# A hybrid decoder step on one core: the kept rows of the cache copied in eight DMAs behind heads 4 to 11, instead of one behind head 7

## The chip, the cores and the metric

The kernel runs on one core of one Trainium2 chip. The time is the device time of that core in microseconds (us), the median of several runs. Engines are named as the profile names them: PE (TensorE), PEld (its weight loads), DVE (VectorE), ACT (ScalarE), POOL (GpSimd), SP (SyncE, which here only issues DMAs). Heads are counted as in the code, from 0, so the twelfth head is head 11.

## The reference, cut to what matters

One step of a decoder of two layers over 512 prompt tokens and 8 x 8 sample tokens. The first layer is a gated linear recurrence with 16 heads, the second a sliding-window attention over one shared K/V. The part that the change is about is the last output: the K/V cache of the eight sample sequences (8 x 128 rows of 512 numbers), shifted by the eight new rows.

```python
def reference(...):
    hp, sp = hgrn2_layer(hp, s_zero, ...)          # layer 0, prompt: 16 heads, 128 x 128 states
    hs, ss = hgrn2_layer(hs, state_hgrn[0], ...)   # layer 0, sample
    kv_p = shared_kv(hp, norm_kv, w_kv)
    kv_s = shared_kv(hs, norm_kv, w_kv)
    ...                                            # layer 1: attention over kv_p, kv_s and the cache
    kv_window_sample = jnp.concatenate([cache_kv_window, kv_s], axis=1)[:, -128:]
```

Of each sequence 120 rows (240 KB) of `cache_kv_window` stay, 8 rows up in the output; they are copied from DRAM to DRAM and nothing in the kernel reads the copy.

## The kernel before, in words

**Stages.** The first layer works head by head. `head_main(h)` multiplies the normed tokens by four 1024 x 128 blocks of `w_in_a` (products `pf`, `pq`, `pi`, `pg`, each of 48 matmuls 128 x 288 on PE, line 233) and ends with the transposes `pvt` and `pvs` (lines 649 and 655). `head_rec(h)` does the recurrence of head h: small matmuls `pa` and `smg`, transposes `pkt` and `pks`, state products `pu`, the chain of states `S` (ACT, then three times DVE, line 856), outputs `poT` and `psO`, sample states `pus`. `woven` writes `head_rec(h)` between the products of `head_main(h + 1)`. Where h is 4, 8 or 12, eight output products `po` of the four heads before (`out_product`, four weight blocks, 24 x 2 matmuls for each product) stand ahead of them.

**Weights.** Every block goes through `split_weights`: one DMA of 512 KB into one of three buffers `raw` (line 198), a cast to `whi` on ACT (line 205), the difference `wlo` on DVE (line 209), then the matmuls. A `raw` buffer is free again when its `wlo` is made.

**What sets the order.** The code gives dependences and priorities. A planner of the framework fixes each engine's instruction order when the kernel is built, with its own estimate of how long every instruction and every DMA takes. On the chip each engine then works through that order and waits where an operand is late. All DMAs of the first layer are issued by SP in one queue, in order; their ends are told by eight semaphores in turn, so an issue can carry a wait for an older DMA that used the same semaphore.

**The copy.** In `head_rec`, after the store of the head's prompt state (`kept`, line 860), head 7 (`CACHE`) issues one DMA (line 864) for the kept rows of all eight sequences, `co[:, : P - DL, :]` from `ci[:, DL:, :]`. `tc.issue_after(kept.ins)` places it right behind the store on SP. After it stand the loads of the next sample states `S0` (line 868, three half tiles of 256 KB) and the stores of the finished ones (line 924).

Of the kernel before, what the change touches and what calls it, by code (L numbers as in the profile page):

```python
# [19 lines left out]
P = 128  # L20
# [3 lines left out]
DB = 8  # L24
DL = 8
# [28 lines left out]
EXTRA = 4  # L54
LAG = 2
SGP = True
CACHE = 7
W = 192
SILU_POOL = True
SCALE = "vpvp"  # L60
# [23 lines left out]
def yoco_kernel(  # L84
# [26 lines left out]
    act, dve, pool, pe, sp = nc.scalar, nc.vector, nc.gpsimd, nc.tensor, nc.sync  # L111
# [416 lines left out]
    ci = cache_kv_window.rearrange("b s k g d -> b s (k g d)")  # L528
    co = kvw_sample.rearrange("b s k g d -> b s (k g d)")

    with ExitStack() as actx:
# [153 lines left out]
        def head_rec(h, st, outs):  # L685
# [172 lines left out]
                        )  # L858
                    Ss.append(S)
            kept = sp.dma_start(st_prompt[0, 0, h], Ss[-1])  # L860
            if h == CACHE:

                with tc.issue_after(kept.ins):
                    sp.dma_start(co[:, : P - DL, :], ci[:, DL:, :])
            S0 = []
            for half in range(2):
                t = wk.tile([P, 4, P], F32, tag="S0", name=f"S0{half}_{h}", bufs=3)
# [94 lines left out]
        for h in range(NH):  # L962
            nxt, chunks, n = {}, [], 0
            if h % 4 == 0 and h:
                chunks.append(out_product(w_out_a, h - 4, outs))
                outs = []
                n += 8
            if h + 1 < NH:
                chunks.append(head_main(h + 1, nxt))
                n += 12  # L970
            else:
                chunks.append(out_product(w_out_a, NH - 4, outs[:FILL]))
                n += 8
            woven(head_rec(h, st, outs), itertools.chain(*chunks), n)
            for make in {5: (prompt_mask,), 6: (sample_mask,), 7: (sink_rows,)}.get(h, ()):
                make()
            st = nxt
# [600 lines left out]
```

## Time and profile before

| what | value |
|---|---|
| time, median of 3 runs | 1152.77 us (1152.27 to 1153.73) |
| time of the profiled execution | 1152.44 us |
| its span, first to last instruction | 1150.6 us |
| mean granted TensorE clock | 0.987 |
| PE busy | 1105.9 us (96%) |
| DVE busy | 857.6 us (75%) |
| ACT busy | 749.4 us (65%) |
| DMA traffic | 123.19 MB, mean 107 GB/s |

The span is the profiled execution from its first to its last instruction; its time is 1.8 us longer. The start of `pvt` (line 649) closes one head's `head_main` on PE, so the time from one `pvt` to the next is a period of the first layer, and two periods that do the same work can be held against each other. A granted clock of 1.00 is 2.4 GHz, and the lower of the two levels is 1.2 GHz.

### The profile page before, as it was taken

To read this page: it belongs to the slowest core of one execution; us is meant where nothing else is said; L and a number is where in the kernel's file an instruction comes from. 1 tells how busy PE (TensorE), PEld (TensorE's weight loads), DVE (VectorE), ACT (ScalarE), POOL (GpSimd) and SP (SyncE) were. 2 spreads that over 40 slices of the span, in tenths; PEclk is the share of its full clock that TensorE was granted. 3 is DMA by queue.
4 is the path that set the end of the run, shared out by engine and by line. 5 is a ranking of instruction groups with operands and counts; after the bars stand their busy time and mean duration, and the time that the engine had idled before them with its cause. 6 is when DMAs were issued, how large, how long until landed. Compare 5 with 4: busy or idle time off the path is not lost.

```text
span 1150.6 us, 27472 instructions
## 1 busy us (share of the span) xinstructions
PE 1105.9 (96%) x10937; PEld 1072.6 (93%) x10937; DVE 857.6 (75%) x2090; ACT 749.4 (65%) x1748; POOL 265.9 (23%) x311
## 2 busy tenths in 40 slices
PE   5999999999999999999999989899999999999997
PEld 4999999998999899999999979899999998999996
DVE  8897777399985498875597887666676767576676
ACT  6677765367673467773566655678866876777665
POOL 1122221021221032121122143332332242232220
PEclk7999999999999999999999999999999999999998
DMA  5332333223233433323323223655545555554552
GB/s 157 93 113 78 104 94 113 77 79 108 71 118 107 122 87 110 89 76 107 96 71 110 86 77 92 143 137 117 132 114 126 129 128 134 126 127 113 127 111 83
DMA packets 168010, 123.19 MB, mean 107 GB/s; under 512 B 4665, under 2 KB 158314, under 8 KB 167850
## 3 DMA queue, kind: packets, MB, share of 16 engines
q1 hardware_dynamic: 160970, 96.26, 28.4%
q0 software_dynamic: 6912, 25.17, 11.6%
q8 instruction: 86, 1.41, 0.5%
q14 instruction: 42, 0.34, 0.1%
HBM read 84.06 MB, written 14.16 MB: 85 GB/s over the span
## 4 chain that ended last, share of the span: by engine, by line
PE 51%; DVE 6%; ACT 3%; issue 1%; DMA 1%; POOL 0%; DVEq 0%; POOLq 0%; ACTq 0%
PE pbg L216 8%; PE pbq L216 8%; PE po L216 6%; PE po L233 4%; PE pg L233 3%; PE pf L233 3%; PE pi L233 3%; PE pq L233 2%; PE sc L1103 2%; PE pkv L216 2%; PE pav L1186 1%; PE pz L216 1%; PE pa L802 1%; PE ptr L1154 1%; DMA wlo_o<-raw_o 1%
## 5 line engine op out<-in xcount | busy, mean ns | idle before, releaser
L205 ACT CAST whi_a<-raw_a 128x1024 fp32r<-128x1024 f32 x64 | 67.1, 1049 | 66.8 <-PE po L233 32.3
L209 DVE TENSOR_TENSOR wlo_a<-raw_a,whi_a 128x1024 fp32r<-128x1024 f32 x64 | 81.8, 1284 | 24.6 <-issue 23.2
L611 POOL TENSOR_TENSOR Xl<-Xl 128x72 f32<-128x72 f32 x80 | 49.6, 649 | 207.0 <-DVE Xl L608 205.7
L643 POOL TENSOR_TENSOR sg<-sg,lg 128x576 f32<-128x576 f32 x16 | 26.2, 1638 | 279.3 <-ACT lg L576 279.3
L1132 ACT ACTIVATE P<-P,st 128x192 f32<-128x192 f32 (+2 forms) x128 | 54.1, 424 | 38.4 <-DVE st L1127 38.3
L1141 POOL TENSOR_SCALAR P<-P,st 128x192 f32<-128x192 f32 (+1 forms) x64 | 47.9, 754 | 93.6 <-DVE st L1134 76.8
L443 DVE TENSOR_TENSOR hT<-hT,po 128x576 f32<-128x576 f32 x32 | 24.1, 754 | 51.0 <-PE po L233 50.7
L233 PE MATMUL po<-oh,whi_o 128*128 128x288 f32 x256 | 42.8, 302 | 4.4 <-ACT whi_o L205 1.9
L216 PE MATMUL po<-ohb,wlo_o 128*128 128x288 f32 x224 | 41.1, 297 | 2.2 <-DMA wlo_o<-raw_o 2.1
L667 POOL TENSOR_TENSOR vb<-vst,bmask 128x512 fp32r<-128x512 f32 x32 | 36.7, 1166 | 26.7 <-DVE vst L663 13.8
L216 PE MATMUL po<-ohb,whi_o 128*128 128x288 f32 x224 | 42.0, 302 | 0.2
L216 PE MATMUL pbq<-xhi,wlo_bq 128*128 128x256 f32 (+1 forms) x256 | 39.9, 297 | 2.4 <-DMA wlo_bq<-raw_bq 2.4
L233 PEld LDWEIGHTS po<-oh,whi_o 128*128 128x128 f32 x256 | 35.9, 188 | 6.4 <-ACT whi_o L205 2.2
L216 PE MATMUL po<-olb,whi_o 128*128 128x288 f32 x224 | 41.4, 298 | 0.5 <-DVE olb L1400 0.4
L233 PE MATMUL po<-ol,whi_o 128*128 128x288 f32 x256 | 41.4, 299 | 0.0
L233 PE MATMUL po<-oh,wlo_o 128*128 128x288 f32 x256 | 41.1, 298 | 0.0
L216 PE MATMUL pbq<-xhi,whi_bq 128*128 128x256 f32 (+1 forms) x256 | 40.5, 300 | 0.0
L216 PE MATMUL pbg<-xhi,whi_bg 128*128 128x288 f32 x256 | 40.5, 300 | 0.0
L216 PE MATMUL pbq<-xlo,whi_bq 128*128 128x256 f32 (+1 forms) x256 | 39.3, 296 | 0.0
L233 PE MATMUL pf<-xhi,wlo_a 128*128 128x288 f32 x256 | 37.5, 299 | 1.8 <-DVE wlo_a L209 1.8
L216 PE MATMUL pbg<-xhi,wlo_bg 128*128 128x288 f32 x256 | 39.1, 295 | 0.0
L233 PE MATMUL pf<-xhi,whi_a 128*128 128x288 f32 x256 | 39.1, 303 | 0.0
(390 smaller groups left out, 3676.7 us busy)
## 6 DMA issues: line engine op xcount, KB each, us to landing
raw_a<-in_w_in_a_dram SPq DMA_DIRECT2D x64, 512.0 KB
S<-in_state_hgrn_dram SPq DMA_DIRECT2D x32, 256.0 KB
out_dram<-S SPq DMA_DIRECT2D x32, 256.0 KB
raw_o<-in_w_out_a_dram SPq DMA_DIRECT2D x16, 512.0 KB
raw_bq<-in_w_in_b_dram SPq DMA_DIRECT2D x16, 512.0 KB
raw_bg<-in_w_in_b_dram SPq DMA_DIRECT2D x16, 512.0 KB
wlo_bq<-raw_bq POOLq DMA_DIRECT2D x16, 512.0 KB, 4.7
wlo_bg<-raw_bg POOLq DMA_DIRECT2D x16, 512.0 KB, 4.8
```

The lines of the kernel that those rows point to most:

```text
L205: act.copy(hi[:, :n], raw[:, :n])
L209: eng.tensor_tensor(lo[:, r], raw[:, r], hi[:, r].bitcast(F32), ALU.subtract)
L216: pe.matmul(pm[:, : c1 - c0], w[:, k * width + w0 : k * width + w0 + P], x(k)[i][:, c0:c1], start=n == 0, stop=n == len(terms) - 1,)
L233: pe.matmul(pm[:, j, :HN], w[:, k * width + c0 : k * width + c0 + P], x(k, j), start=n == 0 and k == 0, stop=n == 2 and k == nk - 1,)
L443: dve.tensor_add(h2, h2, ps2(pm))
L611: pool.tensor_tensor(X8[:, :, j : j + 1], X8[:, :, j : j + 1], X8[:, :, k : k + 1], ALU.add)
L643: (pool if SGP else dve).tensor_tensor(sg, sg, l, ALU.mult)
L667: pool.tensor_tensor(t, view(vst.bitcast(F32), [[0, 4], [1, P]], off=half * P), view(bmask, [[1, 4], [0, P]]), ALU.mult,)
L802: pe.matmul(pa[32 * j : 32 * j + ns, c, t0 : t0 + nt], keys[:, c * P + s0 : c * P + s0 + ns], queries[:, c * P + t0 : c * P + t0 + nt], st ...
L1103: pe.matmul(sc[:, hf, k0[hf] :], QS[pr][:, 2 * n + hf, :], kk[:, g, ks], start=q == 0, stop=q == 1)
L1132: act.activation(x, x, AF.Exp, bias=st[:, a : a + 1], accum_out=st[:, 8 + a : 9 + a])
L1141: (pool if e == "p" else dve).tensor_scalar(x, x, st[:, 8 + a : 9 + a], None, ALU.mult)
```

## The change

`CACHE` becomes 4, and each head from 4 to 11 copies one sequence: 120 rows of 2 KB, 240 KB, in the same place behind its own `kept`. Eight DMAs of 240 KB take the place of one of 1920 KB; the bytes are the same.

```diff
-CACHE = 7
+CACHE = 4
...
             kept = sp.dma_start(st_prompt[0, 0, h], Ss[-1])
-            if h == CACHE:
+            if CACHE <= h < CACHE + DB:
                 with tc.issue_after(kept.ins):
-                    sp.dma_start(co[:, : P - DL, :], ci[:, DL:, :])
+                    sp.dma_start(co[h - CACHE, : P - DL, :], ci[h - CACHE, DL:, :])
```

The order of the instructions moves with it. SP's queue behind the state store of head 7, before (`raw_o` and `raw_a` are weight blocks of `w_out_a` and `w_in_a`, `S_8` and `S_9` sample states of heads 8 and 9; a row is line, operation, target, source, shape):

```order
L860 DMA out_dram<-S_7_4648 128x128
L864 DMA out_dram<-in_cache_kv_window_dram 8x4x15360
L924 DMA out_dram<-S_7_4652 128x4x128
L924 DMA out_dram<-S_7_4654 128x4x128
L198 DMA raw_o_3_5118<-in_w_out_a_dram 128x4x256
L198 DMA raw_a_1_5223<-in_w_in_a_dram 128x8x128
L860 DMA out_dram<-S_8_5286 128x128
L868 DMA S_8_5291<-in_state_hgrn_dram 128x4x128
L198 DMA raw_a_0_5329<-in_w_in_a_dram 128x8x128
```

And after:

```order
L860 DMA out_dram<-S_7_4651 128x128
L864 DMA out_dram<-in_cache_kv_window_dram 16x3840
L924 DMA out_dram<-S_7_4655 128x4x128
L198 DMA raw_o_3_5121<-in_w_out_a_dram 128x4x256
L924 DMA out_dram<-S_7_4657 128x4x128
L868 DMA S_8_5295<-in_state_hgrn_dram 128x4x128
L868 DMA S_9_5883<-in_state_hgrn_dram 128x4x128
L198 DMA raw_a_1_5226<-in_w_in_a_dram 128x8x128
L198 DMA raw_a_0_5333<-in_w_in_a_dram 128x8x128
```

Before, head 8's second half state is loaded only behind head 8's own `L860`; after, both state loads and the next weight blocks stand ahead of it. ACT's queue from the third output weight block of that period on, before (`kt` and `ks` are copies of `pkt` and `pks`, `on` the squares of the head's output):

```order
L205 CAST whi_o_2_5022<-raw_o_2_5020 128x1024
L835 COPY kt_5251<-pkt_5246 128x512
L841 CAST ks_5256<-pks_5253 128x256
L854 COPY S_8_5280<-pu_5275 128x128
L900 ACTIVATE on_5370,rs_5371<-poT_5352 128x128 x4
L205 CAST whi_o_3_5120<-raw_o_3_5118 128x1024
L205 CAST whi_a_1_5225<-raw_a_1_5223 128x1024
```

And after:

```order
L205 CAST whi_o_2_5025<-raw_o_2_5023 128x1024
L205 CAST whi_o_3_5123<-raw_o_3_5121 128x1024
L205 CAST whi_a_1_5228<-raw_a_1_5226 128x1024
L205 CAST whi_a_0_5335<-raw_a_0_5333 128x1024
L835 COPY kt_5254<-pkt_5249 128x512
L841 CAST ks_5259<-pks_5256 128x256
L205 CAST whi_a_2_5435<-raw_a_2_5433 128x1024
L854 COPY S_8_5283<-pu_5278 128x128
```

The cast of the fourth output block moves from behind head 8's recurrence to the place right behind the third. PE's queue in the same period, before, where the whole recurrence of head 8 stands in one piece ahead of the seventh output product `po_6`:

```order
L813 MATMUL smg_5190<-KL_4890 32x64 x2
L833 MATMUL pkt_5246<-ident,KQ_4401 128x128 x4
L839 MATMUL pks_5253<-ident,kd_4900 128x128 x2
L848 MATMUL pu_5275<-vt_4842,kt_5251 128x128 x4
L875 MATMUL poT_5352<-vt_4842,att 128x128 x4
L879 MATMUL psO_5357<-vs_360,atts_358 128x128
L882 MATMUL psO_5357<-S_8_5289,Qz_356 16x128 x2
L893 MATMUL poT_5352<-S_8_5280,KQ_4401 128x128
L893 MATMUL poT_5352<-S_8_5282,KQ_4401 128x128
L893 MATMUL poT_5352<-S_8_5284,KQ_4401 128x128
L911 MATMUL pus_8_5422<-vb_8_4853,ks_5256 128x512
L233 MATMUL po_6_5124<-oh_3259,whi_o_3_5120 128x288 x2
```

And after, where the eight output products are done and the products of `head_main(9)` lie between the steps of the recurrence:

```order
L233 MATMUL po_7_5198<-oh_4797,wlo_o_3_5124 128x288 x2
L233 MATMUL pf_5232<-xhi,whi_a_1_5228 128x288 x16
L833 MATMUL pkt_5249<-ident,KQ_4404 128x128 x4
L839 MATMUL pks_5256<-ident,kd_4903 128x128 x2
L233 MATMUL pf_5232<-xlo,whi_a_1_5228 128x288 x16
L848 MATMUL pu_5278<-vt_4845,kt_5254 128x128 x4
L233 MATMUL pf_5232<-xhi,wlo_a_1_5229 128x288 x16
L233 MATMUL pq_5339<-xhi,whi_a_0_5335 128x288 x16
L875 MATMUL poT_5356<-vt_4845,att 128x128 x4
```

Instructions are neither added nor taken away on PE, DVE, ACT or POOL. Outside heads 8 and 9 their order is what it was; from `pvt` of head 8 to `pvt` of head 10 it is now, row for row but for the numbers in the names, the order that heads 12 and 13 have in both kernels.

## Rows read from the trace of the kernel before

**Rows 1.** The page: busy time of each engine and its share of the span.

```profile
PE 1105.9 (96%) x10937; PEld 1072.6 (93%) x10937; DVE 857.6 (75%) x2090; ACT 749.4 (65%) x1748; POOL 265.9 (23%) x311
```

**Rows 2.** Stretches from one `pvt` to the next: busy us per engine, clock, DMA.

```profile
core 0: us, PE busy (x) PEld busy (x) DVE busy (x) ACT busy (x) POOL busy (x), PEclk, DMA share, GB/s
186.17:245.27 59.10, 59.10 (x609) 58.23 (x608) 33.50 (x59) 26.88 (x57) 6.50 (x8) 1.00 0.30 87
245.27:283.86 38.59, 36.32 (x417) 34.51 (x416) 35.41 (x65) 24.52 (x54) 7.77 (x10) 0.96 0.32 92
353.04:416.91 63.87, 61.48 (x609) 59.72 (x608) 32.26 (x57) 26.18 (x56) 6.39 (x8) 0.97 0.34 97
416.91:453.85 36.94, 34.50 (x417) 32.97 (x416) 35.56 (x61) 24.75 (x55) 9.48 (x8) 1.00 0.32 92
453.85:487.54 33.69, 33.69 (x418) 32.82 (x416) 27.74 (x53) 23.91 (x54) 6.53 (x8) 1.00 0.34 97
521.24:580.34 59.10, 59.10 (x610) 58.23 (x608) 33.47 (x59) 26.86 (x57) 6.50 (x8) 1.00 0.30 87
580.34:615.66 35.32, 34.03 (x417) 32.80 (x416) 32.53 (x59) 24.45 (x54) 8.25 (x8) 1.00 0.35 100
```

**Rows 3.** PE's instructions in time: start us, us, instruction, idle before and releaser.

```profile
353.04 0.60 PE L649 MATMUL pvt<-ident,iT 128*128 128x128 f32 x4
...
376.43 1.16 PE L848 MATMUL pu<-vt,kt 128*128 128x128 f32 x8 [0.46 <-ACT kt L835]
...
382.06 1.32 PE L233 MATMUL po<-oh,whi_o 128*128 128x288 f32 x8 [1.93 <-ACT whi_o L205]
383.22 2.06 PE L233 MATMUL po<-ol,whi_o 128*128 128x288 f32 x8
385.08 1.95 PE L233 MATMUL po<-oh,wlo_o 128*128 128x288 f32 x8
386.87 1.22 PE L233 MATMUL po<-oh,whi_o 128*128 128x288 f32 x8
```

**Rows 4.** One stretch of 4 us, columns as in rows 2.

```profile
382.00:386.00 4.00, 3.94 (x20) 3.94 (x21) 2.36 (x2) 0.96 (x2) 0.00 (x0) 0.66 0.73 210
```

**Rows 5.** ACT's instructions in time, columns as in rows 3.

```profile
380.95 1.06 ACT L205 CAST whi_o<-raw_o 128x1024 fp32r<-128x1024 f32 x1
...
467.80 1.05 ACT L205 CAST whi_a<-raw_a 128x1024 fp32r<-128x1024 f32 x1 [1.45 <-PE pq L233]
```

**Rows 6.** PE's waits from 416.9 to 453.9 us: total us, times, longest.

```profile
PE pf L233 <- DVE wlo_a L209: 1.4, 1, 1.4
PE poT L893 <- DVE S L856: 1.0, 2, 0.7
```

**Rows 7.** PE's waits from 580.3 to 615.7 us.

```profile
PE pa L802 <- issue: 1.1, 1, 1.1
PE pf L233 <- DVE wlo_a L209: 0.2, 1, 0.2
```

**Rows 8.** DVE's instructions in time, the same product in heads 9 and 13.

```profile
423.24 2.06 DVE L780 TENSOR_TENSOR KQ<-KQ,E 128x1024 f32<-128x1024 f32 x1
...
583.18 1.23 DVE L780 TENSOR_TENSOR KQ<-KQ,E 128x1024 f32<-128x1024 f32 x1
```

**Rows 9.** SP's DMA issues in time: start us, us, instruction.

```profile
342.21 0.81 SPq L864 DMA_DIRECT2D out_dram<-in_cache_kv_window_dram  x1
...
442.81 0.36 SPq L860 DMA_DIRECT2D out_dram<-S  x1
447.89 0.38 SPq L924 DMA_DIRECT2D out_dram<-S  x1
449.02 0.38 SPq L198 DMA_DIRECT2D raw_a<-in_w_in_a_dram  x1
...
557.22 0.36 SPq L860 DMA_DIRECT2D out_dram<-S  x1
559.13 0.37 SPq L198 DMA_DIRECT2D raw_a<-in_w_in_a_dram  x1
```

**Rows 10.** SP's waits over the whole span, the one for an older store.

```profile
SPq L868 <- DMA out_dram<-S: 42.5, 17, 4.3
```

## The prediction

> **What bounds the kernel now.** The page's first part first: PE is busy for 1105.9 of 1150.6 us, 96% [rows 1], so in most of the span only less PE work would help, and what can be won by a new order is PE's idle and slow time. This change touches the first layer alone. There I cut PE's timeline at the start of `pvt`, which ends each head's products, and read the periods as a table [rows 2]. Three periods hold a head and eight output products (`pvt` of head 4 to 5, 8 to 9, 12 to 13). The first and the third take 59.10 us, PE busy in all of it at clock 1.00. The second takes 63.87 us, at a mean clock of 0.97, for the same work. The periods behind them (5 to 6, 9 to 10, 13 to 14) take 38.59, 36.94 and 35.32 us; an undisturbed one (10 to 11) takes 33.69, all of it PE. So the stage in which the copy stands, behind head 7, is the one place of the first layer where PE works in a period of its own kind, and the loss against its twins is 63.87 - 59.10 = 4.77 us.
>
> Where PE lost it [rows 3]: 0.46 us before `pu`, for `kt` on ACT; then 1.93 us before the seventh output product, for the cast `whi_o`. Behind that idle time two groups of eight matmuls take 2.06 and 1.95 us where the next takes 1.22, together 1.57 us more, and the granted clock from 382 to 386 us is 0.66, a mix of its two levels, 2.4 and 1.2 GHz [rows 4]. That is 3.96 of the 4.77 us. The rest, 0.81, I leave with the piece from `pkt` to `pus`, where nothing lies between the dependent steps. The cast that PE waited for starts at 380.95 with no idle time noted before it [rows 5]: ACT was not waiting for the weights to land, it came to that cast late because four squares of head 8 stand ahead of it in its queue. So the loss is one of order, not of traffic: the planner took the copy of 1920 KB for long, placed head 8's second state load and the fourth output block late, and put the recurrence of head 8 in one piece ahead of the last two output products.
>
> **The change part by part.** *The order of heads 8 and 9.* After the change it is, on PE, DVE, ACT and POOL, the order of heads 12 and 13, whose times are in the table. Head 8's period should then take the 59.10 us that both its twins take: 4.77 us less.
>
> Head 9's period is 36.94 us now: PE waits 1.4 us for a `wlo_a` of DVE and 1.0 us for the chain of S [rows 6]. DVE is busy in it for 35.56 us, against 32.53 in head 13's period [rows 2], and one product that is the same instruction takes 2.06 us here and 1.23 there [rows 8]: what stands beside it on another engine differs. With head 13's order I take head 13's period as the model, 35.32 us. In it PE waits 0.2 us for `wlo_a`, and 1.1 us for "issue", for nothing that the profile shows [rows 7]. Head 9's period has no such wait [rows 6], and PE's instructions ahead of it are the same in number after the change, so I take it as belonging to that place in PE's instruction stream and leave it out: 35.32 - 1.1 = 34.2 us. The bounds of this term: with the issue wait there too 35.3; as head 5's period, whose order on DVE differs, 38.59; as an undisturbed one 33.69. I take 34.2, 2.7 us less than now, since nothing in the order differs from the row it comes from.
>
> *The copies.* One issue of 0.81 us on SP [rows 9] goes, eight come. I bound one from above by the same 0.81 us, though it moves an eighth, and from below by 0.36, the store ahead of it in the other heads: 2.9 to 6.5 us of SP in all. SP is not on the path. What stands behind a copy on SP is a state store, 5.1 us after `L860` in most heads (442.81 to 447.89), or, in heads 4 and 8, a weight load 1.9 us after it (557.22 to 559.13, head 12, the same order) [rows 9]; both gaps are longer than the issue. The bytes: the same 1920 KB cross the same engines, an eighth at a time, and behind the one big copy, issued at 342.21, PE's first noted wait is that of 0.46 us 34 us later [rows 3, 9], so an eighth of it I cost at nothing. What hides a late weight load is the depth of the three `raw` buffers: the load issued at 449.02 goes into a buffer that two other blocks stand ahead of, and its cast starts at 467.80 [rows 5, 9], 18.8 us later. If that cover were gone, each copy would cost up to its 0.81 us, 6.5 us in all.
>
> Four of the eight copies carry a wait for an older DMA on their semaphore, and while SP holds one, the stores and loads behind it stand. The nearest row is SP's wait of a state load for a store just issued: 42.5 us in 17 times, 2.5 us each, 4.3 at the longest [rows 10]. The older DMA of a copy lies several issues back, so I expect none of it; 4.3 us would still be far inside 18.8.
>
> The Trainium skill speaks against the change: DMA: Bandwidth & Descriptors, section "Measured (HBM→SBUF, 128 partitions, SWDGE, issued from GpSimd)", wants DMAs of 1 MiB and more, and its "Anatomy of one DMA" puts a fixed 2.0 us on each (fitted on another issue path). By it seven more DMAs would be an estimated 14 us, if anything waited for their ends. No row here shows a reader of the copy, so I add nothing for it.
>
> *Elsewhere* the order on each engine is the same but for the copies on SP, and heads 4 to 7 and 10 to 15 and the second layer should keep their times.
>
> **The sum**, against the profiled execution's own 1152.44 us: 1152.44 - 4.77 - 2.7 = 1144.97, call it 1145.0. The median of the runs shown is 0.33 us above that execution, so I forecast 1145.3 us, 7.5 us or 0.65% faster.
>
> **The rivals.** *Only head 8 is mended.* Head 9's period may be DVE's own: head 5's, which is fuller, and head 9's both have PE waiting for S. For it: DVE was busy 35.56 of 36.94 us. Against it: head 13's order ran with 32.53. At head 9's present length the time is 1152.77 - 4.77 = 1148.0; at head 5's 38.59 it is 1152.77 - 4.77 + 1.65 = 1149.65.
>
> *The copies take the gain back.* Each would have to sit on the path with about its issue, 0.81 us: 1145.3 + 6.5 = 1151.8, no change that can be measured. For it: SP is one queue in order, and every weight block of the layer passes behind a copy. Against it: the 18.8 us of cover.
>
> *Slower: a copy stops SP.* The place is line 864 behind `kept`: while it waits for its semaphore, everything behind it on SP stands, and then loads behind a copy land late. The page's fixed cost per DMA would come out in this way. It decides from the point at which the wait eats the 18.8 us less the load's own landing, or the smaller cover of a state load. Priced at the 2.5 us of the row above for each of eight heads: 1145.3 + 20 = 1165.3. For it: only that such waits exist. Against it: the longest seen is 4.3 us.
>
> *The change doesn't do what it says.* The order is fixed at build and stands in the rows of the section on the change, so what is open is only whether the same order gives the same times in another place.
>
> **How the numbers follow.** The forecast, with or without the issue wait in head 9 (1145.3 or 1146.4), 0.76. Only head 8 mended 0.12. The gain taken back 0.08. Slower 0.04. The lower end: head 9's period as the undisturbed 33.69 is 0.5 us below the forecast, runs of the kernel lie up to 0.5 below their median, and the 0.33 between execution and median may not hold: 1144.0. The upper end takes in the rival that mends only head 8, to 1149.7. A measurement of this kernel can tell about 0.2%, 2.3 us, from no change, so faster means below 1150.5: the first two cases, 0.88; same 0.08; slower 0.04.
>
> **What would show it.** In the profile after: `pvt` of head 8 to 9 in 59.1 us without a wait of PE for `whi_o` and at clock 1.00 (first term); `pvt` of 9 to 10 in 34 to 35.5 us, DVE busy about 32.5 and the product of rows 8 near 1.2 us (second term); eight issues of line 864 of 0.4 to 0.8 us, with no wait on SP above 5 us behind them and no new wait of PE for `raw` blocks in heads 4 to 11 (the copies' cost); heads 4 to 7 with the periods they have. I am wrong if head 8's period stays above 60 us though its order is that of head 12, since then something besides the order held it, or if PE waits in heads 5 to 7, where only the copies are new.

## The result

The kernel after takes 1146.55 us, median of 6 runs (1145.78 to 1148.26); the runs of before beside it 1152.52 us. The ratio is 0.9942, with a 95% interval of 0.9931 to 0.9953: 6 to 7 us, 0.6% faster. The forecast was 1145.3 us in a range of 1144.0 to 1149.7. The profiled execution took 1145.94 us.

The page of the kernel after, its span and the engines' busy time, as [rows 1]:

```profile
span 1144.1 us, 27476 instructions
PE 1101.7 (96%) x10937; PEld 1069.6 (93%) x10937; DVE 854.9 (75%) x2090; ACT 749.4 (65%) x1748; POOL 265.3 (23%) x311
```

The periods of the first layer, from one `pvt` to the next, columns as in [rows 2]; heads 4, 5, 6, 8, 9, 10, 12 and 13:

```profile
186.14:245.23 59.09, 59.09 (x609) 58.22 (x608) 33.48 (x59) 26.91 (x57) 6.51 (x8) 1.00 0.31 91
245.23:283.82 38.59, 36.31 (x417) 34.45 (x416) 35.41 (x65) 24.46 (x54) 7.76 (x10) 0.96 0.34 98
283.82:319.32 35.50, 34.26 (x417) 32.93 (x416) 33.60 (x77) 23.02 (x53) 6.67 (x8) 1.00 0.34 97
352.98:412.07 59.09, 59.09 (x609) 58.22 (x608) 33.42 (x59) 26.84 (x57) 6.51 (x8) 1.00 0.32 91
412.07:446.18 34.11, 33.91 (x417) 32.79 (x416) 32.27 (x59) 24.33 (x54) 8.23 (x8) 1.00 0.38 109
446.18:479.87 33.69, 33.69 (x417) 32.82 (x416) 27.57 (x53) 23.75 (x54) 6.56 (x8) 1.00 0.36 101
513.53:572.62 59.09, 59.09 (x610) 58.22 (x609) 33.50 (x59) 26.93 (x57) 6.50 (x8) 1.00 0.30 88
572.62:607.98 35.36, 34.06 (x417) 32.83 (x416) 32.56 (x59) 24.49 (x54) 8.24 (x8) 1.00 0.35 100
```

Head 8's period fell from 63.87 to 59.09 us, PE busy in all of it at clock 1.00; head 9's from 36.94 to 34.11. Heads 4, 5, 12 and 13 are where they were, though six of these eight periods now hold a copy. PE's waits in head 9's period, which stand against [rows 6], are down to this one line:

```profile
PE pf L233 <- DVE wlo_a L209: 0.2, 1, 0.2
```

Head 13 keeps the wait for "issue" of [rows 7], and head 9 has none, as the prediction took it. ACT's casts of the third and the fourth output block in head 8's period (start us, us, instruction, idle before and releaser):

```profile
359.12 1.05 ACT L205 CAST whi_o<-raw_o 128x1024 fp32r<-128x1024 f32 x1 [2.40 <-PE po L233]
365.47 1.05 ACT L205 CAST whi_o<-raw_o 128x1024 fp32r<-128x1024 f32 x1 [5.30 <-PE po L233]
```

The fourth starts at 365.47, where it started at 380.95 in [rows 5], and it is ACT that waits for PE to give a buffer back. The product of [rows 8] in head 9 is down to the time it had in head 13:

```profile
414.92 1.23 DVE L780 TENSOR_TENSOR KQ<-KQ,E 128x1024 f32<-128x1024 f32 x1
```

The copies: the eight issues of line 864 on SP (shortest, median and longest in ns, first and last start), and SP's waits of a state load for a store, as [rows 10]:

```profile
L864 SPq DMA_DIRECT2D out_dram<-in_cache_kv_window_dram x8: 515/516/600, 222.5 to 502.7; - x8
SPq L868 <- DMA out_dram<-S: 41.4, 18, 3.7
```

An issue of 240 KB takes 0.52 us where the one of 1920 KB took 0.81 [rows 9], and this wait did not grow; none is listed for the copies themselves (line 864).

### The profile page after: what moved, and what is told of

It is laid out like the page before. It is cut to its first block, busy times and chain, and to the rows that moved or that the text cites. A ratio compares the mean times of both kernels' runs of the same rounds, so it can differ in the third digit from the quotient of the medians.

```text
span 1144.1 us, 27476 instructions
## 1 busy us (share of the span) xinstructions
PE 1101.7 (96%) x10937; PEld 1069.6 (93%) x10937; DVE 854.9 (75%) x2090; ACT 749.4 (65%) x1748; POOL 265.3 (23%) x311
## 4 chain that ended last, share of the span: by engine, by line
PE 77%; DVE 10%; ACT 6%; issue 2%; POOL 1%; DMA 1%; DVEq 0%; ACTq 0%; POOLq 0%
PE pbg L216 9%; PE po L233 8%; PE pf L233 7%; PE pg L233 7%; PE pi L233 7%; PE pbq L216 7%; PE pq L233 6%; PE po L216 6%; PE pa L802 2%; PE sc L1103 2%; PE pkv L216 2%; PE pav L1186 1%; PE pu L848 1%; PE pz L216 1%; PE poT L893 1%
## 5 line engine op out<-in xcount | busy, mean ns | idle before, releaser
L1107 DVE CUSTOM_DVE_ANT_0 P<-sc,amask 128x192 f32<-128x192 f32 (+2 forms) x128 | 36.4, 328 | 3.6 <-PE sc L1103 3.2
L216 PE MATMUL pbg<-xlo,whi_bg 128*128 128x288 f32 x256 | 39.1, 294 | 0.0
```

Source lines behind the costliest of these rows:

```text
L216: pe.matmul(pm[:, : c1 - c0], w[:, k * width + w0 : k * width + w0 + P], x(k)[i][:, c0:c1], start=n == 0, stop=n == len(terms) - 1,)
L1107: dve.tensor_tensor_reduce(Pt[:, pr, hf, k0[hf] :], sc[:, hf, k0[hf] :], amask[:, k0[hf] :], 0.125, NEG, ALU.add, ALU.max, accum_out=st[:, ...
```

## The experiments

Two explanations stood against each other: the loss of before was one of order (the planner, seeing a long copy behind head 7, moved heads 8 and 9), or one of traffic (1920 KB in one DMA hold the DMA engines, and something of heads 8 and 9 comes late). Each ratio is to runs of before taken beside that run; their medians lie between 1151.82 and 1152.98 us, so times of two rows can differ by a microsecond for that alone, and ratios are the better comparison. "Periods" are head 8's and head 9's, `pvt` to `pvt`, where no other heads are named.

| run | time, us | ratio to before (95%) | periods, us |
|---|---|---|---|
| after | 1146.55 | 0.9942 (0.9931 to 0.9953) | 59.09, 34.11 |
| e1, no copy | 1146.91 | 0.9951 (0.9939 to 0.9963) | 59.09, 34.13 |
| e2, eight small copies behind head 7 | 1153.10 | 1.0004 (0.9995 to 1.0012) | 63.95, 36.98 |
| e3, one big copy behind head 11 | 1152.81 | 0.9997 (0.9986 to 1.0008) | heads 12, 13: 63.86, 36.90 |
| e4, after again | 1146.21 | 0.9942 (0.9928 to 0.9956) | 59.09, 34.13 |
| e5, four behind head 7 | 1147.30 | 0.9953 (0.9939 to 0.9966) | 59.10, 34.11 |
| e6, six behind head 7 | 1153.26 | 0.9999 (0.9991 to 1.0008) | 63.88, 36.96 |
| e7, five behind head 7 | 1147.53 | 0.9953 (0.9941 to 0.9966) | 59.07, 34.13 |
| e8, before again | 1155.04, one run | | 64.02, 36.96 |
| e9, masks moved | 1139.62 | 0.9888 (0.9874 to 0.9903) | heads 5, 6: 34.09, 33.69 |
| e10, one big copy behind head 15 | 1147.54 | 0.9963 (0.9950 to 0.9976) | 59.09, 34.09 |

**e1: no copy.**

```diff
-            if CACHE <= h < CACHE + DB:
-                with tc.issue_after(kept.ins):
-                    sp.dma_start(co[h - CACHE, : P - DL, :], ci[h - CACHE, DL:, :])
```

> The kernel after without the copy: the 120 kept rows of each sequence are not written. The order of the instructions on every engine is that of the kernel after. Theory (the loss of before was one of order, and the eight small copies are hidden): 1146.5 us, as after, within 1 us; periods of heads 8 and 9 of 59.1 and 34.1 us. Rival (the eight copies cost their issue on the path): up to 6.5 us faster than after, 1140 us.

It is no faster than after or e4, which ran beside it: the intervals overlap, and the periods agree to 0.02 us. The eight copies are hidden. The bound of 6.5 us for them is out.

**e2: the small copies, all behind head 7.**

```diff
-            if CACHE <= h < CACHE + DB:
+            if h == 7:
                 with tc.issue_after(kept.ins):
-                    sp.dma_start(co[h - CACHE, : P - DL, :], ci[h - CACHE, DL:, :])
+                    for bb in range(DB):
+                        sp.dma_start(co[bb, : P - DL, :], ci[bb, DL:, :])
```

> Eight copies of 240 KB each, as after, but all eight behind head 7. The order on PE, DVE, ACT and POOL is then, row for row, that of the kernel before. Theory (order): as before, 1152.5 us, head 8's period 63.9 us with a wait of PE of 1.9 us for whi_o. Rival (the form of the one big DMA, 32 long pieces, is what hurt): near after, 1146.5 us.

The whole loss is back with DMAs of the form that after uses. The periods of heads 8 and 9, and PE's waits in the first of them:

```profile
353.13:417.08 63.95, 61.56 (x610) 59.80 (x608) 32.28 (x57) 26.20 (x56) 6.42 (x8) 0.97 0.31 89
417.08:454.06 36.98, 34.50 (x417) 32.94 (x416) 35.59 (x62) 24.75 (x55) 9.49 (x8) 1.00 0.32 93
...
PE po L233 <- ACT whi_o L205: 1.9, 1, 1.9
PE pu L848 <- ACT kt L835: 0.5, 1, 0.5
```

The two waits are those of [rows 3], to a tenth.

**e3: the big copy behind head 11.**

```diff
-            if CACHE <= h < CACHE + DB:
+            if h == 11:
                 with tc.issue_after(kept.ins):
-                    sp.dma_start(co[h - CACHE, : P - DL, :], ci[h - CACHE, DL:, :])
+                    sp.dma_start(co[:, : P - DL, :], ci[:, DL:, :])
```

> The one copy of 1920 KB, as before, but behind head 11. The planner then disturbs heads 12 and 13 as it did heads 8 and 9 before, and heads 8 and 9 have the order of after. Theory (order): head 12's period about 63.9 us instead of 59.1, head 13's 1 to 2 us longer, the time 1152 us. Rival (head 8's place was special, for instance by the masks that DVE makes in heads 5 to 7): heads 12 and 13 lose less than half of that, the time below 1149 us.

The loss goes along to heads 12 and 13, of the same size, and heads 8 and 9 have the short periods (59.09 and 34.09 us):

```profile
513.35:577.21 63.86, 61.47 (x609) 59.71 (x608) 32.20 (x57) 26.12 (x56) 6.39 (x8) 0.97 0.33 96
577.21:614.11 36.90, 34.47 (x418) 32.99 (x417) 35.52 (x62) 24.77 (x55) 9.63 (x8) 1.00 0.33 94
```

**e5, e6, e7: four, six and five of the eight small copies behind head 7**, the others one each behind other heads. This changes one size; the bytes are the same in all. With four the planner's order in heads 8 and 9 is that of after, with six that of before.

```diff
-            if CACHE <= h < CACHE + DB:
+            for bb in {4: (0,), 5: (1,), 6: (2,), 8: (3,), 7: (4, 5, 6, 7)}.get(h, ()):
                 with tc.issue_after(kept.ins):
-                    sp.dma_start(co[h - CACHE, : P - DL, :], ci[h - CACHE, DL:, :])
+                    sp.dma_start(co[bb, : P - DL, :], ci[bb, DL:, :])
```

The table of e6 is `{4: (0,), 5: (1,), 7: (2, 3, 4, 5, 6, 7)}`, that of e7 `{4: (0,), 5: (1,), 6: (2,), 7: (3, 4, 5, 6, 7)}`.

> Four of the small copies (960 KB) behind head 7, the other four one each behind heads 4, 5, 6 and 8. The planner's order on PE, ACT and POOL is still that of after, on DVE but for one neighbouring pair. Theory (order): 1146.4 us as after, head 8's period 59.1 us. Rival (the bytes behind head 7 are what costs, in proportion): half of the loss, 1149.5 us.

> Six of the small copies (1440 KB) behind head 7, one each behind heads 4 and 5. The planner's order on PE, DVE, ACT and POOL is now, row for row, that of before. Theory (order): the whole loss, 1152.6 us, head 8's period 63.9 and head 9's 36.9 us. Rival (bytes in proportion): three quarters of it, 1151 us, and a smooth step from the run with four.

> Five of the small copies (1200 KB) behind head 7, one each behind heads 4, 5 and 6. The planner's order is between the two: on PE the transposes pkt and pks of head 8 and one smg step go ahead of the last output product, the rest of the recurrence stays between the products of head 9. Theory (order): what costs is the recurrence in one piece and the late cast, and neither is here: 1146 to 1147 us. Rival (bytes in proportion): 1150 us.

Head 8's and 9's periods, with four:

```profile
354.72:413.82 59.10, 59.10 (x609) 58.23 (x608) 33.48 (x59) 26.88 (x57) 6.51 (x8) 1.00 0.33 95
413.82:447.93 34.11, 33.90 (x418) 32.79 (x417) 32.36 (x59) 24.35 (x54) 8.22 (x8) 1.00 0.36 102
```

With five:

```profile
353.09:412.16 59.07, 59.07 (x609) 58.20 (x608) 33.57 (x59) 26.78 (x57) 6.50 (x8) 1.00 0.32 91
412.16:446.29 34.13, 33.93 (x417) 32.82 (x416) 32.29 (x59) 24.33 (x54) 8.22 (x8) 1.00 0.36 102
```

With six:

```profile
353.35:417.23 63.88, 61.49 (x610) 59.73 (x609) 32.25 (x57) 26.18 (x56) 6.41 (x8) 0.97 0.30 85
417.23:454.19 36.96, 34.49 (x417) 32.98 (x416) 35.57 (x62) 24.75 (x55) 9.48 (x8) 1.00 0.32 93
```

240 KB more behind head 7 change the first period by -0.03 us from four to five and by +4.81 us from five to six. That is a switch and no price per byte, and the planner's order switches at the same step. The run with five also tells which part of the order costs: there the transposes of head 8 already stand ahead of the last two output products (six products of 24 matmuls each lie before them in the trace, not only ahead of the last, as the expectation has it), and that alone costs nothing. What costs comes with six, the recurrence in one piece and the fourth cast behind it. These two were not taken apart.

**e10: the big copy behind head 15**, the edit of e3 with 15.

> The one copy of 1920 KB behind head 15, with the first layer's order as in after; only at the turn to the second layer does the order differ, by one weight block of the K/V product. Theory (bytes in one piece cost nothing where the order stays good): the last pvt near 642 us, the time 1146 to 1148 us. Rival (the one big copy costs by its traffic, some 5 us, wherever it runs): 1151 us.

SP's issue of it is the 0.81 us of [rows 9], behind the last `pvt` (start us, us, instruction):

```profile
656.39 0.36 SPq L860 DMA_DIRECT2D out_dram<-S  x1
656.80 0.81 SPq L864 DMA_DIRECT2D out_dram<-in_cache_kv_window_dram  x1
```

The last `pvt` starts at 642.25 us, where after has 641.67, and the stretch behind it takes 502.56 us, where after has 502.46. The time is 0.9963 of before, 4.3 us less: the 5 us that the rival asked for are not there. It is no clean test of the traffic, though. The order at the turn is not that of after, and PE has a wait there that after does not have, for a K/V weight block (total us, times, longest):

```profile
PE pkv L216 <- ACT whi_kv L205: 2.0, 1, 2.0
```

The ratio leaves room for a cost of some 2 us against after (0.9963 and 0.9942). Against e3 this is the same DMA four heads later, and some 4 us less by the ratios, 5 by the times.

**e4 and e8: after and before again**, unchanged, for a second profile of each.

> The kernel after, unchanged, for a second profile of it. In the first profile the stretch at the turn to the second layer (K/V products) took 1.6 us more than before, with a lower clock later in it. Theory (the place at which the clock falls there differs from execution to execution): this profile may show either form, and the first layer repeats to 0.1 us. Rival (the change itself lengthens this stretch): the same 1.6 us again, a PE wait of 1.5 us for xlo included.

> The kernel before, unchanged, for a second profile of it. Its first profile spent 10.4 us on the stretch at the turn to the second layer in which five profiles of other kernels spent 12.0, one of them with the very order of before. Theory (execution to execution): 12.0 us here too, or either value. Rival (the change lengthens it): 10.4 us again.

They are about the stretch in which the first profiles did not fit the sum; the next section has them.

**e9: another move in the order, a version that beats both.** In after, heads 5 and 6 have the longest periods of a head without output products (38.59 and 35.50 us), and DVE makes the masks there. The scratch tiles and the masks are the same, only the place moves:

```diff
-            for make in {5: (prompt_mask,), 6: (sample_mask,), 7: (sink_rows,)}.get(h, ()):
+            for make in {4: (prompt_mask,), 8: (sample_mask,), 12: (sink_rows,)}.get(h, ()):
```

> The kernel after, with the making of the attention masks on DVE moved: the prompt's mask from behind head 5 to behind head 4, the sample's from 6 to 8, the sinks' from 7 to 12, that is into the three periods with output products, in which DVE is busy 33 of 59 us. The order on PE and ACT stays. Theory (head 5's and 6's periods are long since the masks fill DVE there): head 5's period from 38.6 or 37.1 to 34 to 35.5 us, head 6's from 35.5 or 37.4 to 33.7, the 59.1 us periods unchanged, 1141 us. Rival (these periods are long whatever DVE does): 1146.4 us, as after.

The periods of heads 4, 5 and 6:

```profile
186.89:245.98 59.09, 59.09 (x610) 58.22 (x609) 35.37 (x65) 26.93 (x57) 7.02 (x10) 1.00 0.31 91
245.98:280.07 34.09, 33.90 (x418) 32.78 (x417) 32.25 (x59) 24.34 (x54) 8.22 (x8) 1.00 0.38 110
280.07:313.76 33.69, 33.69 (x417) 32.82 (x416) 27.56 (x53) 23.74 (x54) 6.56 (x8) 1.00 0.36 104
```

Head 4's period takes the prompt's mask in without a loss, DVE going from 33.5 to 35.4 of 59.1 us. Heads 5 and 6 take 67.78 us together, 6.3 less than the 74.1 of after (38.59 and 35.50), and the kernel 1139.62 us, 1.1% less than before and 6 to 7 us less than after (6 by the ratios, 7 by the times).

## Why the prediction was right, and where it was off

**Head 8's term** was forecast as 4.77 us; the periods give 63.87 - 59.09 = 4.78. The reading behind it, order and not traffic, is what e2, e5, e6 and e7 show: up to 1200 KB behind head 7 without the bad order cost nothing that can be seen (e5, e7), and the bad order without the big DMA costs all (e2, e6). All runs with the bad order also have 1440 KB or more behind one head, so by the runs alone a limit of traffic between 1200 and 1440 KB would do as well. The trace of before decides against it. The fourth output block is issued at 349.55, and in the 20 us ahead of PE's wait for its cast the DMA engines stand all but idle, with a busy share of 0.01 (an issue as in [rows 9], a stretch as in [rows 2]):

```profile
349.55 0.44 SPq L198 DMA_DIRECT2D raw_o<-in_w_out_a_dram  x1
...
360.00:380.00 20.00, 19.54 (x297) 18.33 (x295) 7.21 (x12) 1.42 (x5) 0.03 (x1) 1.00 0.01 2
```

So the block had landed long before ACT cast it at 380.95; e2, e3 and e6 have the same share in the same place. The clue was that cast, with no idle time noted ahead of it: ACT had its operand and was late by its queue. The prediction puts this on the four squares ahead, which take 1 us. The larger part lies before them, where ACT itself waits for PE to come to the recurrence of head 8 (columns as in [rows 5]):

```profile
375.79 0.58 ACT L835 COPY kt<-pkt 128x512 f32<-128x512 f32 x1 [15.56 <-PE pkt L833]
```

In after the fourth cast runs inside the time that ACT spends idle here, at 365.47.

**Head 9's term** was forecast as 2.7 us, 34.2 with the issue wait left out. It is 36.94 - 34.11 = 2.83. The bound of 38.59 that the prediction took from head 5's period holds slow clock, as the last section shows. All profiles with the good order of head 9 have 34.09 to 34.13 there, and head 13, where its own order is the good one, 35.2 to 35.6 with the wait, so this wait does belong to a place in PE's instruction stream.

**The copies** cost nothing, as forecast; e1 is the test. Head 4, where a weight load stands right behind the copy, keeps its 59.09 us. By the fixed 2.0 us that the Trainium skill puts on each DMA (DMA: Bandwidth & Descriptors, "Anatomy of one DMA", fitted on another issue path), eight copies would make after slower than e1 by an estimated 16 us, if something waited for their ends. There is no such difference here (1146.55 and 1146.91 us), as the prediction expected for copies that nothing reads. The rival in which a copy stops SP did not show: SP's longest wait of the kind is 3.7 us, and it was 4.3.

**Elsewhere** is the step that was off: heads 4 to 7, 10 to 15 and the second layer "should keep their times". The first layer did. From the last `pvt` (649.35 us before, 641.67 after) to the end of the span it is 501.25 us before and 502.43 after, so 1.2 us of the 7.7 won in the first layer were missing in this pair of profiles, and this is most of the distance from the forecast 1145.3 to 1146.55. It arises at the turn to the second layer, in the first K/V product. Before (start us, us, instruction, idle before and releaser):

```profile
689.58 1.16 PE L1001 MATMUL pkc<-ident,ck 128*128 128x128 f32 x8 [1.94 <-DVE hT L470]
690.43 2.23 PE L216 MATMUL pkv<-xhi,whi_kv 128*128 128x288 f32 x8
692.46 2.11 PE L216 MATMUL pkv<-xlo,whi_kv 128*128 128x288 f32 x8
694.40 0.29 PE L216 MATMUL pkv<-xhi,wlo_kv 128*128 128x288 f32 x1
```

After:

```profile
681.88 1.09 PE L1001 MATMUL pkc<-ident,ck 128*128 128x128 f32 x8 [1.95 <-DVE hT L470]
682.73 1.30 PE L216 MATMUL pkv<-xhi,whi_kv 128*128 128x288 f32 x8
683.86 1.08 PE L216 MATMUL pkv<-xlo,whi_kv 128*128 128x288 f32 x7
686.49 0.40 PE L216 MATMUL pkv<-xlo,whi_kv 128*128 128x288 f32 x1 [1.55 <-DVE xlo L472]
```

And before again (e8):

```profile
690.30 1.09 PE L1001 MATMUL pkc<-ident,ck 128*128 128x128 f32 x8 [1.93 <-DVE hT L470]
691.15 1.30 PE L216 MATMUL pkv<-xhi,whi_kv 128*128 128x288 f32 x8
692.28 1.08 PE L216 MATMUL pkv<-xlo,whi_kv 128*128 128x288 f32 x7
694.90 0.40 PE L216 MATMUL pkv<-xlo,whi_kv 128*128 128x288 f32 x1 [1.54 <-DVE xlo L472]
```

In the first profile of before the slow clock fell on the matmuls for whose last operand `xlo` PE would have waited anyway, and so hid behind that wait; in after, and in before again, these matmuls ran at full speed, PE waited 1.5 us for `xlo`, and the slow clock came after it. So the two forms are not a matter of the change alone: the same kernel shows both. The same work of the three executions, in two stretches each, from `pkc` to the start of the matmuls `ss` and from there to the end of a second group of 24 matmuls of `pkv`; it takes 10.41 us in before, 12.02 in after and 11.99 in before again:

```profile
689.58:694.84 5.26, 5.12 (x26) 4.69 (x26) 5.20 (x5) 1.62 (x3) 2.85 (x2) 0.68 0.39 104
694.84:699.99 5.15, 5.15 (x35) 4.94 (x36) 2.18 (x5) 2.53 (x6) 1.75 (x5) 1.00 0.68 199
...
681.88:687.16 5.28, 3.60 (x26) 3.14 (x26) 5.22 (x5) 1.62 (x3) 2.88 (x2) 1.00 0.38 107
687.16:693.90 6.74, 6.74 (x35) 6.29 (x36) 2.17 (x5) 2.64 (x6) 1.75 (x5) 0.75 0.55 150
...
690.30:695.57 5.27, 3.59 (x26) 3.14 (x26) 5.22 (x5) 1.63 (x3) 2.87 (x2) 1.00 0.38 107
695.57:702.29 6.72, 6.72 (x35) 6.42 (x36) 2.17 (x5) 2.53 (x6) 1.75 (x5) 0.75 0.53 150
```

Of the 1.6 us that after loses here, 0.4 come back later in the second layer. What failed in the prediction is that it took one execution's second layer for the kernel's. Over the profiles the stretch behind the last `pvt` goes from 501.3 to 504.9 us. What stays open: the medians of the first comparison differ by 6.0 us, its ratio stands for some 6.7, and the first layer's gain is 7.7. The second layer may be a little longer by the change itself, through where the clock falls in it, by 1.7 us at the most if the medians are taken. From the last `pvt` to the first output product of the second layer (`po`, line 216) it is 191.4 us in before and in e6, which has the order of before; 192.9 and 193.1 in e8 and e2, which have it too; and 191.9 to 192.8 in the eight other profiles. The short form thus shows in two of four profiles with the order of before and in none of eight others, which is too few to tell.

## What to carry to other kernels

Where a planner sets the order, the price of a DMA is also what the planner does around it: a copy that nobody waits for cost 7.6 us of two heads' periods, by moving their instructions, and nothing that can be seen once it was cut and spread over eight heads. Cut alone, with all eight pieces behind head 7, it cost the same as before (e2). To find such a place, cut the timeline into periods that do the same work and look for the one that is longer than its twins; then ask of the wait in it whether the late engine was waiting for data or was held by what its queue has ahead, and walk that queue back to the instruction that waited longest. The order of a twin that runs well gave the time of the mended one to a tenth of a microsecond, once a wait that stays at the twin's place was taken out, and the same comparison found the next 6 to 7 us, in heads 5 and 6.

## What the runs showed of the hardware that was not expected

Two places show two forms from execution to execution with the same instructions: the turn to the second layer as above, and heads 5 and 6, where the slow clock falls into head 5's period in some profiles (38.59 and 35.50 us in after) and into head 6's in others (37.04 and 37.40 in after again), for nearly the same sum of 74.1 and 74.4. In e5 it falls in both (38.65 and 37.09, in sum 75.7). In both places PE has short waits just ahead of the fall: of 0.4 to 0.7 us for the chain of states in head 5, of 1.5 or 1.9 us at the turn. A comparison of two single profiles can be off by more than a microsecond for that alone.
